# Attention in a two-layer backbone: a head's first scores ahead of the first projection group, and head norms in two buffers

## The chip, the cores and the metric

The kernel runs on one core of one Trainium2 chip, as one launch. The metric is device time in microseconds. One more execution was taken by the hardware profiler; its trace gives the start and end of each instruction on TensorE (PE for matmuls, PEld for weight loads), VectorE (DVE), ScalarE (ACT), GpSimd (POOL) and SyncE (SP, which issues all DMAs here).

## The reference

Two trunk layers, fp32, over 1024 latent and 256 context tokens of width 1024; layer 0 mixes tokens by differential attention, layer 1 by a state-space layer, and each is followed by an MLP. The change lies in layer 0's attention alone:

```python
q_l = apply_rope(heads_qk(q_l), cos, sin) * scale      # 8 heads, each with two 64-wide halves c
k_all = jnp.concatenate([k_c, k_l], axis=1)            # 1280 keys
s = jnp.einsum('bqhcd,bkhcd->bhcqk', q, k)
p = jax.nn.softmax(s, axis=-1)
w = p[:, :, 0] - lam * p[:, :, 1]                      # difference of two softmaxes
o = jnp.einsum('bhqk,bkhe->bqhe', w, v)
return rmsnorm(o, subln_g) * (1.0 - lambda_init)       # norm over each head's 128 outputs
```

Every product that needs fp32 accuracy is made of three reduced-precision ones (`mm3`, L132 to L134) of operands that `split` (L137 on ACT, L138 on POOL or DVE) cuts into a high and a low part.

## The kernel before

The attention phase (`phase_b`) runs over 72 units: 8 heads of 9 units. Unit 0 of a head holds the 256 context queries, which see 256 keys; units 1 to 8 hold 128 latent queries each, which see all 1280 keys. "(h, u)" below is unit u of head h. On PE, DVE, ACT and POOL the order is the order of the program text; on SP a scheduler sets it. Each engine executes in its own order, so an instruction that waits holds up all behind it on its engine.

The steps of one unit:

- `scores` (L517 in unit 0, L523 in the others) write products of queries Q and keys K to PSUM: banks 0 and 1 in unit 0, banks 0 to 4 otherwise.
- `maxima` on DVE (L532, L536) copy the scores to SBUF with their row maximum. `exps` on ACT (L543, L546) take exponentials and row sums, half c = 0 and then c = 1. `combine` on DVE (L554, L555, L557) forms the difference w.
- `w_part` on PE (L564, L569) transposes the w of the *previous* unit in three parts; part 0 goes to bank 5, part 2 to bank 7 where the unit has no projection group, else to bank 5. Part 0 is read by ACT L577 and DVE L578, the others by ACT L582 and, from a copy, POOL L583 and L584.
- `values` (L132 to L134 with 256 columns) multiplies a finished pair of units with V; `pair_out` (ACT L665, POOL L666) stores the result o to DRAM (`od`), `pair_sums` (PE L672, ACT L673) sums its squares.
- `proj_group` computes a sixth of the next head's Q or K: 24 products, a third of them at a time between the parts ("fills"). AHEAD says in which unit; unit 0 has two groups. The first, of context keys, is written out by ACT L464 and DVE L465 (`direct`). The others go through rotary steps: ACT L469, DVE L470, four row-moving DMAs (`FC<-FC`), POOL L475, DVE L478, and a split (ACT L137, DVE L138) whose DMAs store to DRAM (`Qd<-R`, `Kd<-R`). All groups use bank 7. Q and K are loaded back from DRAM (`R<-Qd`, `R<-Kd`); K's second half for the next head is asked for in unit 8, in a piece of 256 columns (128 KB) and one of 1024.

The head norm of a finished head h-1 runs during head h and head h+1. At the end of (h, 5) `norm_rows` transposes the inverse norms (PE L687), copies them (ACT L689) and writes them to DRAM (`rsd<-W`). For the five pairs of query blocks, in units 6, 7, 8, 0 and 1, `norm_load` asks at the start of the unit for the pair's o (`W<-od`) and for its norm rows spread over 128 partitions (`W<-rsd`). `norm_pair` at the *end* of the same unit multiplies them (DVE L697), splits the product (ACT L137, POOL L138, both `W<-W`) and stores it (`on<-W`). There is one set of buffers, in W.

Of the kernel before, what the change touches and what calls it, by code (L numbers as in the profile page):

```python
# [6 lines left out]
F32 = mybir.dt.float32  # L7
F32R = mybir.dt.float32r
# [5 lines left out]
KB = 256  # L14
# [56 lines left out]
class Prog:  # L71
# [369 lines left out]

        return split

    def proj_group(self, h, T, g, wt):

        nc = self.nc
        n, c0 = self.G_TOK[g], (256, 768, 0)[g]
        b = self.qb.next()[:, 0:n]
        scale = 1.0 if T else -0.125
        t = slice(c0 - 256, c0 + 256)  # L450
        hT = self.hT[g]
        q, sw, qc, s = self.rq, self.rs, self.rc, self.stg[:, :, 0:n]

        def product(k):
            return lambda: self.mm3(b, wt[k][0], wt[k][1], hT[0][:, k], hT[1][:, k], k == 0, k == 7)

        def out():
            dst = self.Kd if T else self.Qd
            for c in range(2):
                self.dma(dst[h % 2, c, :, c0 : c0 + n].rearrange("(l r) n -> r l n", l=2),  # L460
                         s[64 * c : 64 * c + 64].bitcast(F32))

        def direct():
            nc.scalar.activation(s[:, 0], b, AF.Copy, scale=scale)  # L464
            nc.vector.scalar_tensor_tensor(s[:, 1], b, scale, s[:, 0].bitcast(F32), ALU.mult, ALU.subtract)  # L465
            out()

        def evac():
            nc.scalar.activation(q, b, AF.Copy, scale=scale)  # L469
            nc.vector.scalar_tensor_tensor(qc, b, scale, self.cosT[:, t], ALU.mult, ALU.mult)  # L470
            for j in range(4):
                self.dma(sw[32 * j : 32 * j + 32], q[32 * (j ^ 1) : 32 * (j ^ 1) + 32])

        def sine():
            nc.gpsimd.tensor_tensor(sw, sw, self.sinT[:, t], ALU.mult)  # L475

        def add():
            nc.vector.tensor_tensor(qc, qc, sw, ALU.add)  # L478

        def store():  # L480
            self.split(s[:, 0], s[:, 1], qc)
            out()

        return [product(k) for k in range(8)], [direct] if g == 2 else [evac, None, sine, add, store]
# [135 lines left out]
    def phase_b(self):  # L620
# [59 lines left out]
            nc.vector.scalar_tensor_tensor(v, v, 1.0 / 128, tmp, ALU.mult, ALU.add)  # L680
            return lambda: self.rsqrt(rs, v)

        nob, nrb = self.wv(4, 256), self.wv(5, 256)
        nhi, nlo = self.wv(6, 256).bitcast(F32R), self.wv(7, 256).bitcast(F32R)

        def norm_rows(h):
            nc.tensor.transpose(pb[0:10, 384:512], hst[:, 2, h], self.ident)  # L687
            rT = nrb[0:10, 0:128]
            nc.scalar.activation(rT, pb[0:10, 384:512], AF.Copy)  # L689
            self.dma(self.rsd[h], rT)  # L690

        def norm_load(h, pair):
            self.dma(nob, self.od[h, :, 256 * pair : 256 * pair + 256])
            self.dma(nrb, self.rsd[h, 2 * pair : 2 * pair + 2].rearrange("a b -> (a b)").partition_broadcast(128))

        def norm_pair(h, pair):
            nc.vector.scalar_tensor_tensor(nob, nob, self.sg, nrb, ALU.mult, ALU.mult)  # L697
            self.split(nhi, nlo, nob, nc.gpsimd)
            for j, t in enumerate((nhi, nlo)):
                self.dma(self.on[h, j, :, 256 * pair : 256 * pair + 256], t.bitcast(F32))  # L700
# [94 lines left out]
        wts = {1: split(1)}  # L795
# [8 lines left out]
        def evac():  # L804
            while ready:
                self.w_evac(*ready.pop(0))

        with self.manual():
            for n in range(72 + 5):
                h, u = units[n] if n < 72 else (8, 9)  # L810
                front = n < 72
                groups = []
                pv = todo.pop(0)[1:] if todo and todo[0][0] == n else None
                late = pv and pv[1]
                parts = 3 if prev and prev[1] else 1 if prev else 0
                if front and n - 6 >= 9 and (n - 6) % 9 < 5 and (n - 6) // 9 < 7:
                    norm_load((n - 6) // 9 - 1, (n - 6) % 9)
                if h == 7 and u > 5:
                    load6(u)
                if front:  # L820
                    K = loaded[h, 'k', 0], loaded[h, 'k', 1]
                    pair = (u + 1) // 2
                    Q = loaded[h, pair]
                    s0 = hst[:, 0, h]
                    p, sn, sm = (p0.next(), p1), self.stat.next(), self.stat.next()
                    if u == 5 and h < 7:
                        load_v(h + 1)
                        load_k(h + 1, 0)
                    if u % 2 == 0 and u < 8 and (h, pair + 1) not in loaded:
                        load_q(h, pair + 1)  # L830
                    if h < 7:
                        groups = [self.proj_group(h + 1, *a, wts[a[0]]) for a in self.AHEAD.get(u, ())]
                    if len(groups) == 2:
                        for f in groups[0][0] + groups[0][1]:
                            f()
                    self.scores(u, Q, K)
                    if u == 8 and h < 7:
                        load_k(h + 1, 1)
                        load_q(h + 1, 0)
                        load_q(h + 1, 1)  # L840
                    self.maxima(u, p, sm)
                if front:
                    if h < 7:
                        if u == 0:
                            qsplit = self.proj_weights(h + 1, 0)
                        if u == 5 and h < 6:
                            ksplit = self.proj_weights(h + 2, 1)
                if 65 <= n < 75:
                    groups = [wo_group(wo_order[n - 65])]
# [7 lines left out]
                for part in range(3):  # L857
                    if part < parts:
                        tb = pb[:, 256:512] if part == 1 else self.bank(7 if part == 2 and not groups else 5)
                        t = self.w_part(prev[1], prev[2], part, tb)  # L860
                        ready.append((*t, part == 0))
                    if not late or part == 2:
                        evac()
                    if part == 1:
                        next_post()
                    if front and part < 2:
                        self.exps(u, part, p, sm, s0, sn)
                    if front and part == 1:
                        self.combine(u, p, s0, sn)
                    if late and part == 1:  # L870
                        evac()
                    if part == 0:
                        todo7, run7 = run7, []
                        for f in todo7:
                            f.pop(0)()
                            if f:
                                run7.append(f)
                    if part == (2 if n < 73 else 0):
                        while sums and sums[0][0] <= n:
                            sums.pop(0)[1]()  # L880
                    for f in fills[part]:
                        f()
# [19 lines left out]
                if 0 < h < 8:  # L902
# [3 lines left out]
                        newton()  # L906
                    elif u == 5:
                        norm_rows(h - 1)
                if h < 8 and n - 6 >= 9 and (n - 6) % 9 < 5 and (n - 6) // 9 < 7:
                    norm_pair((n - 6) // 9 - 1, (n - 6) % 9)  # L910
                if n == 72:
                    self.raw = Ring([self.wv(8, 1024), self.wv(12, 1024)])
                    self.wo_raws = [self.wo_load(3, 0), self.wo_load(0, 1)]
# [520 lines left out]
    def a_out(self, run, p, t):  # L1434
        self.dma(self.A0[run][p], t)
# [762 lines left out]
    def run(self):  # L2198
        tc = self.tc
        pool = lambda name, **kw: tc.tile_pool(name=name, bufs=1, **kw)  # L2200
        with pool("cst") as self.cst, pool("psp", space=bass.MemoryType.PSUM) as psp, \
# [22 lines left out]
            with pool("r0") as rp, pool("fc") as cp:  # L2224
                self.R, self.F = rp.tile([128, 59 * KB], F32R, name="R0"), cp.tile([128, 8 * KB], F32, name="FC")
                with pool("f0") as fp, pool("sp") as sp:
                    self.F0, self.SP = fp.tile([128, 41 * KB], F32, name="F0"), sp.tile([128, 12 * KB], F32, name="SP")
                    self.f0 = lambda off, *dims: self.view(self.F0, off, dims)
                    self.setup()
                    self.lam_setup()  # L2230
                    more = [self.view(self.SP, 4 * i, (1024,)) for i in range(3)]
                    self.raw = Ring([self.wv(4 * i, 1024) for i in range(4)] + [self.f0(24.5 + 4 * i, 1024) for i in range(4)] + more)
                    self.phase_v()
                with pool("r1") as rp, pool("f1") as fp:
                    self.R1, self.F1 = rp.tile([128, 20 * KB], F32R, name="R1"), fp.tile([128, 21 * KB], F32, name="F1")
                    self.phase_b()
                for g in range(3):
                    for j in range(2):
                        self.dbg(f"oT{g}{j}", self.oT[g][j].bitcast(F32))
                if self.stop == "B":  # L2240
                    return
# [69 lines left out]
```

## Time and profile before

| | |
|---|---|
| median of 3 runs | 2927.47 us (2924.79 to 2931.78) |
| profiled execution | 2919.65 us, of it 2917.8 us span |
| mean granted TensorE clock | 0.983 |
| attention phase in the span | from 221.28 us (first L517) to about 877 us |
| PE, DVE, ACT, POOL busy | 94%, 69%, 47%, 36% of the span |

In the rows of the profile, `L132 PE MATMUL PS<-H,R` is line, engine, operation, and what is written from what. `[2.56 <-ACT F L582]` is idle time of that engine before the instruction and what ended it. A row of waits reads: who waited, for whom, total us, times, longest. A row of stretches reads: from:to, us, then busy time of PE, PEld, DVE, ACT and POOL with their instruction counts (or of one engine alone), granted TensorE clock, DMA share, GB/s.

### The profile page before, as it was taken

Reading aid. Unit: us, or ns where it says so; the run is one execution under the profiler, and the core shown is the slowest. Engines: PE = TensorE matmul, PEld = TensorE weight load, DVE = VectorE, ACT = ScalarE, POOL = GpSimd, SP = SyncE. Lnnn points to the kernel's source line nnn. Section 1 sums busy time; section 2 is a strip of 40 time slices with the busy share of each in tenths; the row PEclk is TensorE's granted clock in tenths of the full one; section 3 lists DMA queues with packets and bytes.
Section 4 is the critical chain, followed back from the end, with each engine's and each line's share of the span. In section 5 each row is a group of like instructions: output and inputs, shape, how many; then the busy total and the mean of one; then the engine's idle time right before and its main releaser. Section 6 shows DMA issues by size and latency. Waiting matters only on the chain.

```text
span 2917.8 us, 43645 instructions
## 1 busy us (share of the span) xinstructions
PE 2739.2 (94%) x15201; PEld 2287.3 (78%) x15201; DVE 2021.4 (69%) x2957; ACT 1369.8 (47%) x2556; POOL 1063.4 (36%) x923
## 2 busy tenths in 40 slices
PE   6999999999899999999999999688899899999999
PEld 4787888878777887878877778588788688878887
DVE  5457777777764576767697868699743787758566
ACT  3425655555553753333443435377543643345443
POOL 3314666666653600000020004499310443326324
PEclk9999999999999999999999999899999999999999
DMA  9955555555735448886799988468834254467544
GB/s 299 307 171 159 151 174 166 170 157 152 236 117 166 132 164 314 295 301 221 244 293 278 276 247 253 148 202 276 270 130 131 72 183 157 148 212 254 165 134 141
DMA packets 452010, 588.43 MB, mean 202 GB/s; under 512 B 60622, under 2 KB 297420, under 8 KB 448588
## 3 DMA queue, kind: packets, MB, share of 16 engines
q1 hardware_dynamic: 451788, 585.63, 63.6%
q8 instruction: 120, 1.97, 0.3%
q14 instruction: 102, 0.84, 0.1%
HBM read 398.47 MB, written 182.82 MB: 199 GB/s over the span
## 4 chain that ended last, share of the span: by engine, by line
PE 62%; DMA 12%; DVE 12%; issue 6%; ACT 3%; POOL 3%; SPq 2%; DVEq 0%; POOLq 0%; ACTq 0%
PE PS L132 18%; PE PS L134 17%; PE PS L133 17%; SPq L80 2%; DMA FU<-in_mlp_w 2%; PE PS L523 2%; PE PS L1802 2%; ACT F L546 1%; DMA Ta<-FU 1%; PE PS L1837 1%; DVE H L138 1%; PE PS L569 1%; DVE F L536 1%; DVE R L138 1%; DMA U<-in_mlp_w 1%
## 5 line engine op out<-in xcount | busy, mean ns | idle before, releaser
L132 PE MATMUL PS<-H 128*128 128x512 f32 x1048 | 411.9, 394 | 7.3 <-DVE FD L1609 5.0
L134 PE MATMUL PS<-H 128*128 128x512 f32 x1048 | 409.8, 392 | 1.1 <-DVE H L138 1.1
L133 PE MATMUL PS<-H 128*128 128x512 f32 x1048 | 410.7, 392 | 0.0
L132 PE MATMUL PS<-H,R 128*128 128x512 f32 (+1 forms) x836 | 310.9, 377 | 18.6 <-ACT F L582 13.7
L133 PE MATMUL PS<-H,R 128*128 128x512 f32 (+1 forms) x836 | 303.9, 364 | 1.1 <-POOL H L138 1.1
L134 PE MATMUL PS<-H,R 128*128 128x512 f32 (+1 forms) x836 | 303.3, 363 | 0.0
L132 PEld LDWEIGHTS PS<-H 128*128 128x128 f32 x1048 | 197.7, 189 | 51.8 <-DVE FD L1609 5.3
L134 PEld LDWEIGHTS PS<-H 128*128 128x128 f32 x1048 | 197.7, 189 | 43.9 <-DVE H L138 1.5
L133 PEld LDWEIGHTS PS<-H 128*128 128x128 f32 x1048 | 197.8, 189 | 41.5 <-issue 1.3
L137 ACT ACTIVATE R<-W 128x512 fp32r<-128x512 f32 (+1 forms) x199 | 138.7, 704 | 185.4 <-PE PS L133 112.9
L546 ACT ACTIVATE F<-F,stat 128x1280 f32<-128x1280 f32 x128 | 174.4, 1362 | 84.3 <-DVE F L536 84.1
L132 PE MATMUL PS<-R,H 128*128 128x512 f32 x532 | 212.3, 401 | 1.4 <-ACT R L137 1.4
L133 PE MATMUL PS<-R,H 128*128 128x512 f32 x532 | 209.7, 394 | 0.0
L134 PE MATMUL PS<-R,H 128*128 128x512 f32 x532 | 207.6, 394 | 0.2 <-POOL H L138 0.2
L137 ACT ACTIVATE H<-U 128x640 fp32r<-128x640 f32 x216 | 132.8, 677 | 152.1 <-PE PS L133 114.6
L132 PEld LDWEIGHTS PS<-H,R 128*128 128x128 f32 x836 | 160.5, 193 | 47.8 <-ACT F L582 15.1
L138 DVE TENSOR_TENSOR H<-W,H 128x512 fp32r<-128x512 f32 (+1 forms) x137 | 128.9, 952 | 96.7 <-ACT H L137 95.7
L138 DVE TENSOR_TENSOR H<-U,H 128x640 fp32r<-128x640 f32 x216 | 163.1, 791 | 42.0 <-ACT H L137 42.0
L536 DVE TENSOR_SCALAR_CACHE_REDUCE F<-PS 128x1280 f32<-128x1280 f32 x128 | 185.1, 1483 | 8.6 <-PE PS L523 8.3
L138 DVE TENSOR_TENSOR R<-W,R 128x512 fp32r<-128x512 f32 (+1 forms) x164 | 149.1, 916 | 57.3 <-ACT R L137 49.5
L583 POOL TENSOR_SCALAR R<-F 128x256 fp32r<-128x256 f32 (+1 forms) x128 | 123.8, 967 | 169.9 <-ACT F L582 148.7
L134 PEld LDWEIGHTS PS<-H,R 128*128 128x128 f32 x836 | 160.6, 192 | 26.2 <-POOL R L138 1.0
(488 smaller groups left out, 6830.6 us busy)
## 6 DMA issues: line engine op xcount, KB each, us to landing
W<-in_mlp_w SPq DMA_DIRECT2D x184, 256.0 KB, 3.1
U<-Aa SPq DMA_DIRECT2D x108, 320.0 KB, 4.8
Aa<-FU SPq DMA_DIRECT2D x91, 320.0 KB, 4.6
Ad<-F SPq DMA_DIRECT2D x112, 256.0 KB, 2.6
W<-Ad SPq DMA_DIRECT2D x112, 256.0 KB, 2.7
FU<-in_mlp_w SPq DMA_DIRECT2D x32, 512.0 KB, 6.1
Ta<-FU SPq DMA_DIRECT2D x16, 1024.0 KB, 4.8
recd<-U SPq DMA_DIRECT2D x64, 256.0 KB, 4.5
```

The costliest lines, as they stand in the source:

```text
L80: return self.nc.sync.dma_start(out=out, in_=in_)
L132: mm(out, ah, bh, start=first, stop=False, **kw)
L133: mm(out, ah, bl, start=False, stop=False, **kw)
L134: mm(out, al, bh, start=False, stop=last, **kw)
L137: self.nc.scalar.activation(hi, src, AF.Copy)
L138: (lo_eng or self.nc.vector).tensor_tensor(lo, src, hi.bitcast(F32), ALU.subtract)
L523: mm(self.PS[:, 1280 * c + k0 : 1280 * c + k1], Q[:, c, r, qs], K[c][:, k0:k1], start=r == 0, stop=r == 1)
L536: ts(p[c], self.PS[:, 1280 * c : 1280 * c + 1280], 1.0, None, ALU.mult, ALU.min, accum_out=sm[:, c : c + 1])
L546: nc.scalar.activation(p[c], p[c], AF.Exp, bias=sm[:, c : c + 1], scale=-1.0, accum_out=sn[:, 0:1] if c else s0[:, u + 1 : u + 2])
L569: self.nc.tensor.transpose(tb[:, 128 * (kt - k0) : 128 * (kt - k0) + 128], w[:, 128 * kt : 128 * kt + 128], self.ident)
L583: nc.gpsimd.tensor_scalar(hi, t, 1.0, 0.0, ALU.mult, ALU.add)
L1802: mm(b[:, o : o + 160], X[:, d, i, 64 * j : 64 * j + 128], U[:, 4 * n + i, cols], start=True, stop=True)
```

## The change

1. In unit 0 the head's scores stand first on PE, and the products of the first group follow; that group is written to bank 4 instead of bank 7. Its `direct` step follows `maxima`.
2. The norm's loaded buffers and its split buffers exist twice, the second set in F1 (4.5 KB more per partition). The inverse norms are copied to a place of their own there.
3. The loads of pairs 1 to 4 are asked for one unit earlier, at the start of the unit ahead of that of their `norm_pair`; the load of pair 0 stands at the end of (h, 5), behind `norm_rows`.
4. `norm_pair` moves from the end of its unit to the middle, behind `exps` of c = 1 and ahead of `combine`.

```diff
-    def proj_group(self, h, T, g, wt):
+    def proj_group(self, h, T, g, wt, bank=None):
...
-        b = self.qb.next()[:, 0:n]
+        b = (self.qb.next() if bank is None else bank)[:, 0:n]
...
-        nob, nrb = self.wv(4, 256), self.wv(5, 256)
-        nhi, nlo = self.wv(6, 256).bitcast(F32R), self.wv(7, 256).bitcast(F32R)
+        nbufs = [(self.wv(4, 256), self.wv(5, 256))] + [(self.view(self.F1, 21 + 2 * i, (256,)), self.view(self.F1, 22 + 2 * i, (256,)))
+                                                        for i in range(1)]
+        nsplit = [(self.wv(6, 256).bitcast(F32R), self.wv(7, 256).bitcast(F32R))] + \
+                 [tuple(self.view(self.F1, 23 + i, (256,)).bitcast(F32R) for i in range(2))]
+        (nob, nrb), nbuf = nbufs[0], Ring(range(2))
+        nloaded = []
...
         def norm_load(h, pair):
-            self.dma(nob, self.od[h, :, 256 * pair : 256 * pair + 256])
...
+            i = nbuf.next()
+            nloaded.append(i)
+            self.dma(nbufs[i][0], self.od[h, :, 256 * pair : 256 * pair + 256])
...
         def norm_pair(h, pair):
+            i = nloaded.pop(0)
+            (nob, nrb), (nhi, nlo) = nbufs[i], nsplit[i]
...
-                if front and n - 6 >= 9 and (n - 6) % 9 < 5 and (n - 6) // 9 < 7:
-                    norm_load((n - 6) // 9 - 1, (n - 6) % 9)
+                if front and n - 6 >= 9 and (n - 6) % 9 < 4 and (n - 6) // 9 < 7:
+                    norm_load((n - 6) // 9 - 1, (n - 6) % 9 + 1)
...
-                        groups = [self.proj_group(h + 1, *a, wts[a[0]]) for a in self.AHEAD.get(u, ())]
+                        groups = [self.proj_group(h + 1, *a, wts[a[0]], self.bank(4) if a == (1, 2) else None)
+                                  for a in self.AHEAD.get(u, ())]
+                    self.scores(u, Q, K)
                     if len(groups) == 2:
-                        for f in groups[0][0] + groups[0][1]:
+                        for f in groups[0][0]:
                             f()
-                    self.scores(u, Q, K)
...
                     self.maxima(u, p, sm)
+                    if len(groups) == 2:
+                        groups[0][1][0]()
...
                     if front and part == 1:
+                        if n - 6 >= 9 and (n - 6) % 9 < 5 and (n - 6) // 9 < 7:
+                            norm_pair((n - 6) // 9 - 1, (n - 6) % 9)
                         self.combine(u, p, s0, sn)
...
                     elif u == 5:
                         norm_rows(h - 1)
-                if h < 8 and n - 6 >= 9 and (n - 6) % 9 < 5 and (n - 6) // 9 < 7:
-                    norm_pair((n - 6) // 9 - 1, (n - 6) % 9)
+                        if h < 7:
+                            norm_load(h - 1, 0)
```

More of the change, by code (lines that the diff above doesn't have):

```diff
@@ L681, in norm_calc @@
             return lambda: self.rsqrt(rs, v)
-        nob, nrb = self.wv(4, 256), self.wv(5, 256)
-        nhi, nlo = self.wv(6, 256).bitcast(F32R), self.wv(7, 256).bitcast(F32R)
+        nbufs = [(self.wv(4, 256), self.wv(5, 256))] + [(self.view(self.F1, 21 + 2 * i, (256,)), self.view(self.F1, 22 + 2 * i, (256,)))
[4 more added lines that the diff above has]
+        nloaded = []
         def norm_rows(h):
             nc.tensor.transpose(pb[0:10, 384:512], hst[:, 2, h], self.ident)
-            rT = nrb[0:10, 0:128]
+            rT = self.view(self.F1, 25, (128,))[0:10]
             nc.scalar.activation(rT, pb[0:10, 384:512], AF.Copy)
@@ L692, in norm_load @@
         def norm_load(h, pair):
-            self.dma(nob, self.od[h, :, 256 * pair : 256 * pair + 256])
-            self.dma(nrb, self.rsd[h, 2 * pair : 2 * pair + 2].rearrange("a b -> (a b)").partition_broadcast(128))
+            i = nbuf.next()
+            nloaded.append(i)
+            self.dma(nbufs[i][0], self.od[h, :, 256 * pair : 256 * pair + 256])
+            self.dma(nbufs[i][1], self.rsd[h, 2 * pair : 2 * pair + 2].rearrange("a b -> (a b)").partition_broadcast(128))
         def norm_pair(h, pair):
+            i = nloaded.pop(0)
+            (nob, nrb), (nhi, nlo) = nbufs[i], nsplit[i]
             nc.vector.scalar_tensor_tensor(nob, nob, self.sg, nrb, ALU.mult, ALU.mult)
@@ L2234, in run @@
                 with pool("r1") as rp, pool("f1") as fp:
-                    self.R1, self.F1 = rp.tile([128, 20 * KB], F32R, name="R1"), fp.tile([128, 21 * KB], F32, name="F1")
+                    self.R1, self.F1 = rp.tile([128, 20 * KB], F32R, name="R1"), fp.tile([128, int(25.5 * KB)], F32, name="F1")
                     self.phase_b()
```

## The prediction

> **What bounds the kernel now.** I read the page first, then who waited for whom inside the attention phase, then one head in order of time, engine by engine.
>
> ```profile
> span 2917.8 us, 43645 instructions
> PE 2739.2 (94%) x15201; PEld 2287.3 (78%) x15201; DVE 2021.4 (69%) x2957; ACT 1369.8 (47%) x2556; POOL 1063.4 (36%) x923
> ...
> PE PS L569 <- DVE R L578: 20.2, 15, 2.7
> PE PS L132 <- ACT F L582: 13.7, 6, 2.6
> ...
> DVE W L697 <- DMA W<-rsd: 30.3, 14, 4.4
> ```
>
> PE is the bound, and what can be won is its idle time. In the attention phase it waits 13.7 us for L582: that is the first group, six times, because the previous unit's part 2 still occupies bank 7. The waits for L578 come from DVE, which itself stood 30.3 us before L697 for the norm rows. Both are what the change aims at. The ceiling is thus a few tens of us of 2919.65.
>
> The stretches from (h, 6) to (h+1, 3), for h = 1 to 5 and, last, (6, 6) to (7, 3), hold nearly all of it; the first time in each row is its length:
>
> ```profile
> 348.49:405.69 57.20, 51.88 (x329) 45.70 (x327) 43.78 (x70) 32.47 (x67) 34.75 (x35) 1.00 0.59 173
> 430.84:487.61 56.77, 53.14 (x328) 47.15 (x327) 42.28 (x70) 32.57 (x67) 34.99 (x35) 0.97 0.59 174
> 512.77:570.75 57.98, 53.34 (x329) 47.16 (x328) 43.37 (x70) 32.10 (x67) 34.74 (x35) 0.97 0.57 170
> 595.95:654.00 58.05, 53.16 (x328) 47.13 (x327) 43.45 (x70) 32.58 (x67) 34.79 (x35) 0.97 0.62 171
> 679.19:736.83 57.64, 52.06 (x329) 45.70 (x328) 42.91 (x70) 32.45 (x67) 34.75 (x35) 1.00 0.60 172
> 762.01:824.99 62.98, 47.67 (x275) 41.96 (x274) 43.02 (x68) 32.08 (x64) 35.48 (x34) 0.86 0.79 249
> ```
>
> The first five average 57.5 us. I follow head 1; its PE, in order of time:
>
> ```profile
> 355.51 2.56 PE L523 MATMUL PS<-R,R 128*128 128x512 f32 x12
> 357.91 0.60 PE L569 MATMUL PS<-ident,F 128*128 128x128 f32 x4
> 374.69 0.39 PE L132 MATMUL PS<-H,R 128*128 128x256 f32 x1 [2.56 <-ACT F L582]
> 377.67 1.12 PE L517 MATMUL PS<-R,R 128*128 128x256 f32 x8
> 380.05 0.50 PE L132 MATMUL PS<-H,R 128*128 128x512 f32 x1 [0.83 <-DVE R L465]
> 386.82 2.47 PE L523 MATMUL PS<-R,R 128*128 128x512 f32 x12
> 397.27 0.39 PE L133 MATMUL PS<-R 128*128 128x256 f32 x1 [1.50 <-DVE R L578]
> ```
>
> Unit 7 begins at 355.51, the next head's scores at 377.67, its unit 1 at 386.82. Three waits stand there: 2.56 for bank 7, 0.83 for L465 (the same bank, second group), 1.50 in unit 2.
>
> **The change, part by part.**
>
> *The order in unit 0.* The group loses its wait for bank 7: bank 4 is free once `maxima` of unit 8 are done, ahead of PE's arrival. Gone are 2.56 and 0.83. PE does the same 32 matmuls in the other order, so nothing is added there. What is late next is what the scores need.
>
> *Pair 0 of the norm, the step I weigh most.* Its rows are written at the end of unit 5 and read back in unit 6. The built program has L697 of pair 0 behind the two L536 of unit 6 and ahead of L554. In the kernel before, it came after L578:
>
> ```profile
> 351.59 1.49 DVE L536 TENSOR_SCALAR_CACHE_REDUCE F<-PS 128x1280 f32<-128x1280 f32 x1
> 354.61 0.16 DVE L554 RECIPROCAL stat<-stat 128x1 f32<-128x1 f32 x1 [1.52 <-ACT F L546]
> 356.53 0.69 DVE L578 TENSOR_TENSOR R<-PS,R 128x512 fp32r<-128x512 f32 x1
> 357.24 0.75 DVE L697 SCALAR_TENSOR_TENSOR W<-W,lamc 128x256 f32<-128x256 f32 x1
> 365.71 1.23 DVE L138 TENSOR_TENSOR R<-FC,R 128x512 fp32r<-128x512 f32 x1
> ...
> 604.86 0.58 DVE L697 SCALAR_TENSOR_TENSOR W<-W,lamc 128x256 f32<-128x256 f32 x1 [0.19 <-DMA W<-rsd]
> ...
> 353.61 0.54 SPq L80 DMA_DIRECT2D W<-rsd  x1
> ...
> W<-rsd SPq DMA_DIRECT2D x35, 128.0 KB, 4.0
> ```
>
> The rows' read is issued at 353.61 and, at a median of 4.0 us to landing, is there at about 357.2 to 357.6; head 4's L697, at the same place, still waited 0.19. Nothing in the change brings this read forward: it stands behind the same row-moving DMAs and the same write. So DVE, done with L536 at 353.1, now stands until 357.2, and `combine` of unit 6, queued behind, goes with it. From 357.2: L697 about 0.5, then the 2.6 us that L554 to the end of L578 took (354.61 to 357.22): 360.3. PE's first transposes of unit 7 (357.91) need that w and bank 5, which L578 frees: a new wait of 2.4 us. ACT is held too: the norm's copy stands ahead of L577 and of the L582 behind it, and POOL's L583 follows those.
>
> *What that delays, and the keys.* On POOL and DVE:
>
> ```profile
> 356.10 0.79 POOL L583 TENSOR_SCALAR R<-F 128x256 fp32r<-128x256 f32 x1 [4.99 <-ACT F L582]
> 360.38 1.30 POOL L475 TENSOR_TENSOR FC<-FC,W 128x512 f32<-128x512 f32 x1
> 361.71 1.77 DVE L478 TENSOR_TENSOR FC<-FC 128x512 f32<-128x512 f32 x1 [0.30 <-POOL FC L475]
> ...
> 289.93 1.27 SPq L80 DMA_DIRECT2D Qd<-R  x2
> 291.30 2.74 SPq L80 DMA_DIRECT2D FC<-FC  x4
> 294.14 1.02 SPq L80 DMA_DIRECT2D R<-Kd  x2
> ...
> R<-Kd SPq DMA_DIRECT2D x14, 128.0 KB, 2.3
> ```
>
> L554 moves from 354.61 to about 357.6, hence L577, L582, L583 and L475 by the same 3.0, L478 with them; L697 of pair 1, now ahead of `combine` of unit 7, adds its 0.75: the store split L138 ends at 370.6 instead of 366.9. In the changed program's SP order the 256 key columns that `scores` of unit 0 read stand behind that store and the four FC moves, as they did at head 0 already; at heads 1 to 5 they stood ahead. From store to issue is 4.2 us (289.93 to 294.14), landing 2.3 more: 377.1. PE, 2.4 late, is ready at 372.1 + 2.4 = 374.5. New wait: 2.6 us, in place of the 2.56. Before, the group's products covered that load; now they stand behind the scores.
>
> So scores start at 377.1. Until unit 1 PE has what took 12.1 us (374.69 to 386.82) less the 0.83: 11.3; another head took slightly less, I take 11.1. Unit 1 begins at 388.2, 1.4 late. In unit 2 the 1.50 goes: L578 there is not later, because the L697 that stood ahead of `maxima` is gone, and PE arrives late itself. With DVE's wait for pair 4's rows gone too (the loads are a unit ahead now), unit 3 begins 0.7 earlier than before, averaged over the heads. Five heads: -3.5 us.
>
> *The clock.* A wait also costs afterwards. Consecutive stretches, PE busy first, granted clock second:
>
> ```profile
> 369.70:373.11 3.41, 2.42 (x22) 1.00 0.68 219
> 455.03:458.45 3.42, 1.42 (x12) 1.00 0.72 137
> 458.45:461.86 3.41, 3.41 (x19) 0.50 0.93 279
> ```
>
> PE idle 2.0 of 3.41 us was followed by 3.41 us at half clock; idle 1.0 was not. A wait of 2.5 us, wherever it begins, puts 2.0 into one such stretch about half the time ((3.41 + 2.5 - 4.0) / 3.41 = 0.56). Half clock costs 1.7 us of PE work. In unit 7 the wait for keys hides it; behind that wait nothing does. Half of five: +4.3; the three 0.97 stretches above, hardly longer than the other two, already hold 0.5. Net +3.8. (The Trainium skill, "TensorE: Matmul & The Clock Gate", section "HAM oscillation", warns of idle gaps beyond about 3.4 us alone; by it these waits cost nothing afterwards, and the sum would be 3.8 lower. The trace has half clock after PE waits of 2.5 us, so I charge it.)
>
> *Head 0's start.* There the group ran while Q was loading:
>
> ```profile
> 222.76 1.68 PE L517 MATMUL PS<-R,R 128*128 128x256 f32 x7 [1.13 <-DMA R<-Qd]
> ```
>
> Now it follows: its 2.98 us (374.69 to 377.67 at full clock) come onto PE's path, less about 0.7 of waits of its own that it had there: +2.3. I take that near the 0.83 of its wait for L465 in head 1. Bounds: 0 if the waits of units 1 and 2 absorb it, 4 at half clock.
>
> *Head 0 to 1.* No norm runs there; the group's wait for bank 7 gives way to one for the keys, 294.14 + 2.3 = 296.4, about when bank 7 came free: 0.
>
> *Head 6 to 7.*
>
> ```profile
> 775.13 0.49 DVE L697 SCALAR_TENSOR_TENSOR W<-W,lamc 128x256 f32<-128x256 f32 x1 [4.40 <-DMA W<-rsd]
> 779.10 0.96 PE L569 MATMUL PS<-ident,F 128*128 128x128 f32 x4 [2.72 <-DVE R L578]
> 801.51 0.98 PE L672 MATMUL PS<-lamc,adat 128*128 128x1 f32 x4 [6.44 <-ACT F L582]
> ```
>
> The rows land at 775, so unit 7's wait grows by about 4; in return the 6.44 in head 7's unit 0 shrinks, as its L697 finds its rows. I take 0, within 3 either way: no row shows POOL, busy there, without its waits.
>
> *Sum:* 2.3 - 3.5 + 3.8 = +2.6 us on the profiled execution: 2919.65 + 2.6 = 2922.3. The runs' median, 2927.47, is 7.8 above that execution; I add the same 2.6: **2930 us**.
>
> **The rivals.**
>
> *A: the keys come in time.* DVE's pairs of waits shrink (L697 took 0.49 to 0.75, L478 could run in 0.7 instead of 1.77), or the short key load lands before PE is ready. Then a head saves the 2.6, unit 1 starts early and unit 2's waits vanish entirely: 3.7 a head, 18.5 in all, less 2.3: 2911. For it: the key load has only 2.6 us to make up. Against: it hangs behind a store on DVE that the norm moves back.
>
> *B: the rows also come in time,* so that pair 0 costs nothing: 28 us won, 2899. Against it speaks the 0.19 wait at 604.86; only an earlier read could do it, and the change has none.
>
> *C: slower, by the queue behind the store and the half clock after it.* Each us by which L138 or the FC moves are later holds the keys and all of unit 0 by as much. At one more us per head and half clock behind every wait for keys: 5 + 8.5 - 0.5 - 3.5 + 2.3 = +12: 2939. It decides from the point where keys land later than about 378 in head 1's time. For it: three of six such waits before already led to half clock, and other loads crowd SP there. Against: unit 2's waits still give some back.
>
> **How the numbers follow.** 0.2% is about what a measurement of this kernel can tell from no change: 5.9 us, so 2921.6 to 2933.3 counts as the same. Forecast 0.40, A 0.21, B 0.06, C 0.33. Faster is A and B, 0.27; same 0.40; slower 0.33. The forecast's own range is 2922 to 2934. For eight in ten I leave out B and the far end of C: low, A gives 2911; high, C with head 6 at +3 and 1 for rounding gives 2943.
>
> **What would show it.** Right: L697 of pair 0 idle about 4 us for its rows ahead of L554; PE waiting 2 to 3 us at unit 7's first L569 and again at L517 for `R<-Kd`; no wait of the first group for L582; none of L697 in unit 2. Wrong: PE passing from unit 8 into L517 without a wait (A), or unit 7's transposes on time (B); stretches of head 1 to 5 above 59 us with clock 0.95 or less (C).

## The result, and the profile after

| | before | changed |
|---|---|---|
| median of 20 runs each | 2927.31 us | 2938.30 us |
| ratio to before, 95% interval | | 1.0035 (1.0024 to 1.0047) |
| span of the profiled execution | 2917.8 us | 2931.8 us |
| attention phase, first L517 to the scores of (7, 8) | 653.9 us | 662.3 us |

The changed kernel is slower by 0.35%, about 10 us. The two profiled executions differ by 14.0 us, of which 8.4 lie in the attention phase. What lies outside that phase is the same program, and its part of the span ranges from 2257 to 2277 us over the thirteen kernels profiled here, in no order that follows an edit; so from here on each kernel's profile is read by the length of its attention phase, and its time by the ratio of its runs. Each phase length is that of one execution; how much it varies between executions of one kernel, no run here shows.

The first lines of the changed kernel's page. PE is busy 2.2 us more than before, DVE 6.8 us less: 11.8 of the extra 14.0 us of span are idle time of PE.

```profile
span 2931.8 us, 43649 instructions
...
PE 2741.4 (94%) x15201; PEld 2288.7 (78%) x15201; DVE 2014.6 (69%) x2957; ACT 1367.6 (47%) x2556; POOL 1071.3 (37%) x923
```

Who waited for whom in the attention phase (total us, times, longest; here and below from 221 to 877 us of the trace). L705 is the norm's product, L697 before.

```profile
PE PS L569 <- DVE R L578: 29.7, 14, 7.7
...
DVE F L705 <- DMA F<-rsd: 19.8, 3, 9.6
...
DVE W L705 <- DMA W<-rsd: 12.6, 3, 4.3
...
PE PS L133 <- DVE R L578: 11.5, 6, 3.7
PE PS L517 <- DMA R<-Kd: 11.1, 6, 2.6
...
ACT R L137 <- DMA Kd<-R: 8.9, 5, 2.2
```

The row of the first group's wait for L582 (13.7 us before) is gone. In its place stand 11.1 us for the key load, and L569's wait has grown from 18.6 to 29.7 (the 20.2 of the prediction is for a longer window, 217 to 900). DVE still waits 32.4 us for norm rows (before: 30.3): the second set of buffers has not shortened that, it has left fewer and longer waits (6 for 14), and they stand where `combine` stands behind them.

The stretches from (h, 6) to (h+1, 3), as before: five of them now average 59.4 us (57.5 before), and the last takes 65.43.

```profile
347.33:407.72 60.39, 53.78 (x329) 47.03 (x327) 43.20 (x71) 32.03 (x67) 35.43 (x35) 0.97 0.56 164
432.29:491.32 59.03, 52.03 (x328) 45.76 (x327) 43.18 (x71) 32.04 (x67) 35.44 (x35) 1.00 0.56 168
515.92:575.38 59.46, 53.25 (x328) 46.79 (x327) 43.08 (x71) 32.16 (x67) 35.36 (x35) 0.97 0.58 167
600.01:659.46 59.45, 53.19 (x328) 46.78 (x327) 43.63 (x71) 32.15 (x67) 35.35 (x35) 0.97 0.56 167
684.10:742.88 58.78, 53.24 (x329) 46.96 (x328) 43.17 (x71) 32.02 (x67) 35.40 (x35) 0.97 0.57 168
767.45:832.88 65.43, 49.06 (x275) 42.43 (x274) 45.19 (x68) 31.78 (x64) 37.05 (x34) 0.84 0.78 243
```

Head 1 in the changed kernel, engine by engine (start, duration, what it is, idle time before it and what ended it):

```profile
355.93 0.48 DVE L705 SCALAR_TENSOR_TENSOR W<-W,lamc 128x256 f32<-128x256 f32 x1 [4.00 <-DMA W<-rsd]
356.33 0.16 DVE L554 RECIPROCAL stat<-stat 128x1 f32<-128x1 f32 x1
...
358.99 0.66 PE L569 MATMUL PS<-ident,F 128*128 128x128 f32 x4 [2.08 <-DVE R L578]
...
369.91 1.28 SPq L80 DMA_DIRECT2D Qd<-R  x2
371.29 2.74 SPq L80 DMA_DIRECT2D FC<-FC  x4
374.13 1.26 SPq L80 DMA_DIRECT2D R<-Kd  x2
...
376.56 0.98 PE L517 MATMUL PS<-R,R 128*128 128x256 f32 x6 [2.57 <-DMA R<-Kd]
...
398.32 0.39 PE L133 MATMUL PS<-R 128*128 128x256 f32 x1 [1.63 <-DVE R L578]
```

Read down: DVE stands 4.00 us for pair 0's rows, and L554 of `combine` follows it; PE waits 2.08 for the L578 at the end of that chain; the store `Qd<-R` and the four row moves go out ahead of `R<-Kd`; PE waits 2.57 for those keys; and in unit 2, where the prediction saw no wait, PE still waits 1.63. That last wait has its own chain, on ACT and DVE in unit 1:

```profile
388.66 0.63 ACT L137 ACTIVATE R<-FC 128x512 fp32r<-128x512 f32 x1 [2.21 <-DMA Kd<-R]
...
389.33 0.69 DVE L138 TENSOR_TENSOR R<-FC,R 128x512 fp32r<-128x512 f32 x1 [2.47 <-ACT R L137]
...
390.74 1.48 DVE L536 TENSOR_SCALAR_CACHE_REDUCE F<-PS 128x1280 f32<-128x1280 f32 x1
```

ACT's split L137 of the next store writes the staging buffer `stg`, and there the first group's context keys still lie until their store `Kd<-R` has read them. DVE's half of the split waits for ACT, and unit 1's `maxima` (L536) stand behind it in DVE's order.

### The profile page after: what moved, and what is told of

Read it like the earlier page. It is cut to its first block, busy times and chain, and to the rows that moved or that the text cites. A ratio compares the mean times of both kernels' runs of the same rounds, so it can differ in the third digit from the quotient of the medians.

```text
span 2931.8 us, 43649 instructions
## 1 busy us (share of the span) xinstructions
PE 2741.4 (94%) x15201; PEld 2288.7 (78%) x15201; DVE 2014.6 (69%) x2957; ACT 1367.6 (47%) x2556; POOL 1071.3 (37%) x923
## 4 chain that ended last, share of the span: by engine, by line
PE 63%; DMA 13%; DVE 9%; POOL 5%; issue 4%; ACT 3%; SPq 2%; ACTq 0%; DVEq 0%; POOLq 0%
PE PS L132 18%; PE PS L134 18%; PE PS L133 18%; SPq L80 2%; PE PS L523 2%; PE PS L1815 2%; PE PS L569 1%; PE PS L1850 1%; DMA FU<-in_mlp_w 1%; DMA Ta<-FU 1%; DVE H L138 1%; DMA Kd<-R 1%; ACT F L546 1%; POOL R L583 1%; DVE F L557 1%
## 5 line engine op out<-in xcount | busy, mean ns | idle before, releaser
L137 ACT ACTIVATE R<-W 128x512 fp32r<-128x512 f32 (+1 forms) x199 | 138.8, 705 | 183.3 <-PE PS L133 116.9
L137 ACT ACTIVATE H<-U 128x640 fp32r<-128x640 f32 x216 | 132.7, 677 | 150.8 <-PE PS L133 114.2
L536 DVE TENSOR_SCALAR_CACHE_REDUCE F<-PS 128x1280 f32<-128x1280 f32 x128 | 185.2, 1483 | 8.9 <-PE PS L523 8.3
L133 PEld LDWEIGHTS PS<-H,R 128*128 128x128 f32 x836 | 160.7, 192 | 27.8 <-POOL H L138 6.8
L132 PEld LDWEIGHTS PS<-H,R 128*128 128x128 f32 x836 | 160.4, 192 | 27.1 <-issue 4.1
L134 PEld LDWEIGHTS PS<-H,R 128*128 128x128 f32 x836 | 160.3, 192 | 25.6 <-issue 0.8
```

Of the source, the lines that this page charges most:

```text
L132: mm(out, ah, bh, start=first, stop=False, **kw)
L133: mm(out, ah, bl, start=False, stop=False, **kw)
L134: mm(out, al, bh, start=False, stop=last, **kw)
L137: self.nc.scalar.activation(hi, src, AF.Copy)
L536: ts(p[c], self.PS[:, 1280 * c : 1280 * c + 1280], 1.0, None, ALU.mult, ALU.min, accum_out=sm[:, c : c + 1])
```

## The experiments

The theory held after the comparison, **N**, has two parts: pair 0's product stands ahead of `combine` without its rows, and the 256 key columns come too late for the scores. A third, **G**, was added after the first four kernels below: the group's later place makes its staging buffer come free late. The main rival to N was **S**: putting the scores first exposes the key load whatever the norm does. Phase lengths are from the first L517 to the scores of (7, 8); it is 653.9 in the kernel before. Each kernel's ratio is to runs of the kernel before made beside its own.

| kernel | ratio to before (95%) | phase, us |
|---|---|---|
| changed | 1.0035 (1.0024 to 1.0047) | 662.3 |
| order and bank alone | 1.0004 (0.9987 to 1.0021) | 656.7 |
| norm half alone | 1.0008 (0.9992 to 1.0025) | 659.6 |
| changed, keys early | 1.0050 (1.0033 to 1.0066) | 665.1 |
| changed, rows written a unit earlier | 0.9969 (0.9953 to 0.9985) | 649.1 |
| before, bank 4 alone | 0.9964 (0.9952 to 0.9976) | 644.5 |
| changed, norm a unit later | 0.9919 (0.9907 to 0.9931) | 629.6 |
| changed, own staging | 1.0012 (1.0003 to 1.0020) | 654.9 |
| changed, keys early and own staging | 0.9994 (0.9982 to 1.0005) | 648.2 |
| all three: norm later, keys early, own staging | 0.9905 (0.9882 to 0.9928) | 621.8 |
| the same, inverse norms in one unit | 0.9892 (0.9871 to 0.9912) | 622.0 |
| old order, bank 4, norm later | 0.9921 (0.9896 to 0.9946) | 629.6 |

**The two halves.** First the order and the bank alone, on the kernel before:

```diff
-                        groups = [self.proj_group(h + 1, *a, wts[a[0]]) for a in self.AHEAD.get(u, ())]
+                        groups = [self.proj_group(h + 1, *a, wts[a[0]], self.bank(4) if a == (1, 2) else None)
+                                  for a in self.AHEAD.get(u, ())]
+                    self.scores(u, Q, K)
                     if len(groups) == 2:
-                        for f in groups[0][0] + groups[0][1]:
+                        for f in groups[0][0]:
                             f()
-                    self.scores(u, Q, K)
...
                     self.maxima(u, p, sm)
+                    if len(groups) == 2:
+                        groups[0][1][0]()
```

> The order of unit 0 and bank 4 alone; the norm as in the kernel before. Theory N (the loss comes from the norm half: pair 0's product ahead of combine without its rows, and the later place of the key load on SP that goes with it): the first group's waits in unit 8 (13.7 us in all) and the two of 0.83 go, the 256 key columns stay ahead of the store on SP and land about 368 in head 1's time, so the scores of unit 0 wait for nothing; head 0's start adds 1.9. About 10 to 14 us faster than before, 2913 to 2917. Rival S (scores ahead of the group expose the key load whatever the norm does): a wait of 1.5 to 2.5 us at L517 in each of six heads takes the place of the one removed; 2926 to 2930.

Measured: no difference from before, so both were wrong in part. The time is the one S gave, but its cause is not there: the scores of heads 2 to 6 pass without a wait for keys, because their load stands ahead of the store on SP in this kernel. Theory N fails on the gain. The waits of this kernel, and SP and PE at head 1's end:

```profile
ACT R L137 <- DMA Kd<-R: 20.8, 5, 4.7
...
PE PS L569 <- DVE R L578: 18.0, 13, 2.5
...
PE PS L133 <- DVE R L578: 10.6, 6, 3.3
...
PE PS L523 <- DVE F L536: 8.7, 12, 2.3
...
PE PS L517 <- DMA R<-Kd: 0.9, 1, 0.9
```

```profile
365.78 0.32 SPq L80 DMA_DIRECT2D R<-Kd  x1
367.13 1.27 SPq L80 DMA_DIRECT2D Qd<-R  x2
...
383.59 1.07 PE L523 MATMUL PS<-R,R 128*128 128x512 f32 x4
...
392.36 1.19 PE L523 MATMUL PS<-R,R 128*128 128x512 f32 x4 [2.27 <-DVE F L536]
```

PE reaches unit 1 at 383.59 instead of 386.82, 3.2 us early, and loses it there: unit 2's scores wait 2.27 for unit 1's `maxima`, which follow the split that waits for `Kd<-R`. ACT waits 20.8 us in all for that store, against 8.9 in the changed kernel. G came from these rows and those of the early keys, below.

The norm half alone (the changed kernel with unit 0 as before, and bank 7):

```diff
-                        groups = [self.proj_group(h + 1, *a, wts[a[0]], self.bank(4) if a == (1, 2) else None)
-                                  for a in self.AHEAD.get(u, ())]
+                        groups = [self.proj_group(h + 1, *a, wts[a[0]]) for a in self.AHEAD.get(u, ())]
+                    if len(groups) == 2:
+                        for f in groups[0][0] + groups[0][1]:
+                            f()
                     self.scores(u, Q, K)
-                    if len(groups) == 2:
-                        for f in groups[0][0]:
-                            f()
...
                     self.maxima(u, p, sm)
-                    if len(groups) == 2:
-                        groups[0][1][0]()
```

> The norm half alone (two buffers, loads a unit ahead, the product in the middle of the unit); unit 0 as in the kernel before, the first group on bank 7 and ahead of the scores. Theory N: PE waits 2.1 to 3.6 us at unit 7's first transposes in heads 1 to 5 and 7 to 8 in head 6, the first group's waits of about 2.5 stay, units 3 and 5 give back 0.6 a head and head 7's unit 0 about 5: 5 to 12 us slower than before, 2932 to 2939. Rival S: the norm half costs nothing or gains, 2920 to 2928.

```profile
PE PS L569 <- DVE R L578: 28.3, 14, 8.1
...
PE PS L132 <- ACT F L582: 11.9, 6, 2.8
```

Measured 1.0008, which can't be told from no change: it is the time that S gave, and its interval reaches into N's 5 to 12 us, so the time doesn't decide. N's waits are there, and in the phase they cost 5.7 us. At unit 7 PE waits 19.4 us in six heads (20.8 in the changed kernel), and the first group's wait stays (11.9, before 13.7). No wait for keys appears, since the group's products cover their load. The halves cost 2.8 and 5.7 us of phase, about the change's 8.4 together, but not out of the same waits: the wait for keys (11.1 us) exists only with both, because the order takes away its cover and the norm half its place on SP.

**The keys, taken away.** The 256 columns get a buffer of their own, and their load is asked for in unit 7 instead of unit 8:

```diff
+        kx = self.view(self.R1, 20, (256,))
+
+        def load_kx(h):
+            self.dma(kx.bitcast(F32), self.Kd[h % 2, 1, :, 0:256])
...
+                    if u == 7 and h < 7:
+                        load_kx(h + 1)
...
-                    self.scores(u, Q, K)
+                    self.scores(u, Q, (K[0], kx) if u == 0 and h else K)
```

> The changed kernel with one more buffer of 1 KB per partition: the 256 key columns of the second half that unit 0 reads are loaded into it by a DMA of their own, units earlier; the rest as it is. Theory N with its second part right: the waits at L517 (11.1 us in six heads) go, those at unit 7 stay: 8 to 12 us less than the changed kernel, about 2927 to 2930, level with the kernel before. Rival S: the whole loss goes and more, 2915 to 2925. If the wait only moves to unit 1 or 2: no change from 2938.

```profile
PE PS L569 <- DVE R L578: 29.6, 18, 6.9
...
ACT R L137 <- DMA Kd<-R: 18.0, 5, 4.1
...
PE PS L132 <- ACT FC L670: 5.6, 6, 0.9
...
PE PS L523 <- DVE F L536: 4.4, 10, 1.0
```

The row for L517 is gone, and the time isn't less: the third case named, the wait moves. Unit 0 starts early, ACT waits for the staging 18.0 us instead of 8.9, and in unit 2 PE waits 5.6 us for L670 and 4.4 for `maxima` (0.9 and 0.7 in the changed kernel). A wait of 11.1 us on the engine that bounds was worth nothing by itself. (The Trainium skill, "Perfetto Trace Analysis", section "Optimization Strategy", advises to find the gaps on the bound engine and make what blocks them start sooner. Here that removed the gap and left the time, as the next dependency was due just behind.)

**The rows, in time.** The inverse norms are finished and written one unit earlier:

```diff
                     if u == 3:
-                        newton = norm_calc(h - 1)
+                        norm_calc(h - 1)()
                     elif u == 4:
-                        newton()
-                    elif u == 5:
                         norm_rows(h - 1)
-                        if h < 7:
-                            norm_load(h - 1, 0)
+                    elif u == 5 and h < 7:
+                        norm_load(h - 1, 0)
```

> The changed kernel with the inverse norms finished and written out one unit earlier (end of unit 4 instead of 5), so that pair 0's rows can land before unit 6; pair 0's load stays at the end of unit 5. Theory N: DVE's idle time before pair 0's product goes, with it PE's waits at unit 7 (2.1 to 3.6 us in five heads, 7.7 in head 6, of which 2.7 were there before); the waits at L517 stay near 2: 14 to 19 us less than the changed kernel, 2919 to 2924. Rival S: unit 7 on time but the time lost again at L517, under 5 us less, 2933 to 2938.

```profile
PE PS L691 <- ACT FC L665: 14.9, 6, 2.5
...
PE PS L517 <- DMA R<-Kd: 12.8, 6, 2.7
...
PE PS L569 <- DVE R L578: 2.4, 2, 1.9
```

N confirmed, and a new bill: L569 waits 2.4 us in all instead of 29.7, and DVE waits for no rows. But the transposes of `norm_rows` (L691), now in a unit that also writes out a pair, wait 2.5 us each, 14.9 in all, and the waits for keys are now followed by half clock in all of heads 2 to 6. With that the phase is 649.1, 13 less than changed; in runs it is 0.9969 against 1.0035, about 19.

The other way to the same end is to need the rows later: all five products one unit later.

```diff
-                        if n - 6 >= 9 and (n - 6) % 9 < 5 and (n - 6) // 9 < 7:
-                            norm_pair((n - 6) // 9 - 1, (n - 6) % 9)
+                        if n - 7 >= 9 and (n - 7) % 9 < 5 and (n - 7) // 9 < 7:
+                            norm_pair((n - 7) // 9 - 1, (n - 7) % 9)
```

(and the loads of pairs 1 to 4 likewise)

> The changed kernel with all five products of the norm, and the loads of pairs 1 to 4, one unit later (pair 0's product in unit 7); pair 0's load stays at the end of unit 5. Theory N: the rows have landed, PE's waits at unit 7 (2.1 to 3.6 us, 7.7 in head 6) go; the waits at L517 stay: 14 to 19 us less than the changed kernel, 2919 to 2924, as with the rows written earlier. Rival: pair 0 in unit 7 holds VectorE ahead of the store split, keys come later still, under 8 us less, above 2930.

```profile
PE PS L569 <- DVE R L578: 11.4, 9, 2.1
...
PE PS L517 <- DMA R<-Kd: 10.0, 6, 2.3
```

0.9919, well beyond both expectations: faster than before by 0.8%. The phase is 32.7 us shorter than the changed kernel's, of which the waits at unit 7 are only 20.8 (13.1 in heads 1 to 5, 7.7 in head 6). The expectation left out the clock: PE is at half clock for 22.4 us of the phase here and for 37.5 in the changed kernel. The 17.1 us that began in unit 7 there are all gone, with 2.0 more elsewhere: 15.1 less, an estimated half of that in time, 7.5. Another 3.3 are waits in head 7's unit 2 (1.57 instead of 4.84), 1.1 fewer for keys.

**The bank without the order.** The kernel before, with its first group on bank 4 and still ahead of the scores:

```diff
-                        groups = [self.proj_group(h + 1, *a, wts[a[0]]) for a in self.AHEAD.get(u, ())]
+                        groups = [self.proj_group(h + 1, *a, wts[a[0]], self.bank(4) if a == (1, 2) else None)
+                                  for a in self.AHEAD.get(u, ())]
```

> The kernel before with one edit: the first group of unit 0 goes to bank 4; its products stay ahead of the scores. Theory G (what the order half loses, it loses because the group comes later: the context keys are staged and stored 3 to 4 us later from the one staging buffer, the split of the next store waits for that DMA, VectorE waits for the split and takes unit 1's maxima late): without the new order the staging is earlier, not later, so the waits for bank 7 (15.4 us) go and little comes in their place: 8 to 14 us faster than before, 2911 to 2917. Rival: units 1 and 2 are bound by VectorE in any case, the 2.5 us come back there, under 4 us gained, 2921 to 2925.

0.9964, in G's range. One of the change's two parts in unit 0 is a gain of 0.36%, and the other spends it: the order costs 12 us of phase (656.7 beside 644.5). The wait on the staging agrees with G, at a third of the 20.8 us with the order:

```profile
ACT R L137 <- DMA Kd<-R: 7.1, 3, 2.5
```

**The staging.** The changed kernel with a buffer of its own for the first group's result:

```diff
         q, sw, qc, s = self.rq, self.rs, self.rc, self.stg[:, :, 0:n]
+        if bank is not None:
+            s = self.view(self.R1, 20, (2, 256))
```

> The changed kernel with one more buffer of 2 KB per partition: the first group's result is staged there, so the split of the next store does not wait until it has been written out. Theory G: ScalarE's wait for the key store (2.2 us in head 1), VectorE's 2.5 behind it and PE's 1.6 in unit 2 go: 5 to 9 us less than the changed kernel, 2929 to 2933. Rival: the 1.6 in unit 2 is the chain of maxima, exponentials and combine, timed from unit 1's own scores; it stays, 2936 to 2940.

```profile
PE PS L571 <- DVE R L580: 27.1, 14, 5.9
...
PE PS L519 <- DMA R<-Kd: 14.1, 6, 3.0
...
PE PS L133 <- DVE R L580: 6.0, 6, 3.7
```

Head 3's unit 1 and its first `maxima`:

```profile
471.13 2.49 PE L525 MATMUL PS<-R,R 128*128 128x512 f32 x12
...
472.73 1.49 DVE L538 TENSOR_SCALAR_CACHE_REDUCE F<-PS 128x1280 f32<-128x1280 f32 x1
```

(Lines are two higher here: L571 is L569, L519 is L517, L525 is L523, L538 is L536.) The row of ACT's wait for `Kd<-R` is gone, and unit 2's wait, 1.26 to 1.63 in the changed kernel, falls to 0.23 or 0.24 in heads 2, 3, 5 and 6; in head 4 it is 1.40. `maxima` begin 1.60 us after unit 1's scores in those four heads (472.73 less 471.13), in the changed kernel 2.63 to 3.40. 1.0012 against 1.0035: G holds, the rival doesn't. With the early keys as well:

> The changed kernel with both buffers, the 256 key columns loaded early and the first group's own staging. The early keys alone gave nothing (2939). Theory G: they gave nothing because the staging was next in line; with both the waits at L517 and those of 3.6 us in units 1 and 2 go together: 15 to 20 us less than with the keys alone, 2919 to 2925. Rival: something else in units 1 and 2 binds, no more than 5 us less, 2934 or above.

```profile
PE PS L571 <- DVE R L580: 30.2, 16, 5.5
...
PE PS L133 <- DVE R L580: 7.7, 6, 1.6
```

0.9994 against 1.0050 with the keys alone, 16 us: the keys are worth something once the staging isn't next in line. In part the rival holds too: with the scores this early, 1.6 us in unit 2 come back in four of five heads. ACT no longer waits for the staging there; in head 2 DVE is at work without a gap on unit 0's `combine` and the split until `maxima` begin, 3.2 us after unit 1's scores (391.03 less 387.81), so DVE's own work is now next in line.

**All three, and a version that beats both kernels.**

> The changed kernel with the norm one unit later and both buffers (keys early, own staging). If the three causes add up, the waits at unit 7, at L517 and most of those in unit 2 are gone: against the norm one unit later alone, whose waits at L517 are 1.7 us and in unit 2 1.4 us a head, 6 to 12 us less, 0.988 to 0.990 of the kernel before. Rival (PE is now held in units 1 and 2 by the chain of maxima, exponentials and combine whatever comes first): no more than 3 us less, 0.991.

```profile
PE PS L571 <- DVE R L580: 10.8, 9, 1.7
...
PE PS L133 <- DVE R L580: 9.3, 6, 1.6
```

0.9905 of before lies between the expectation and its rival and can't be told from the 0.9919 of the later norm alone; the phase, 7.8 us shorter, speaks for the expectation. The waits at unit 7 and for keys are gone, those in unit 2 are not: PE still waits 1.6 there in each of heads 2 to 6, and 1.2 in unit 5. For the latter, both steps of the inverse norms were put at the end of unit 3, as in the kernel with early rows, where unit 5 had no wait:

> The same, with both steps of the inverse norms (sum and reciprocal root) at the end of unit 3 instead of units 3 and 4. PE's wait of 1.2 us in unit 5 (before: 1.5), which comes from VectorE's steps at the end of unit 4, goes in six heads: 5 to 7 us less than the kernel without this edit. Rival: it moves to unit 4, no change.

The phase is the same (622.0 and 621.8), and unit 5 waits 1.21 as before: the expectation was wrong. In the kernel with early rows, where that wait was missing, unit 4 was 2.9 us longer (9.9 for 7.0), which is a likely reason that no run here tests. The ratio, 0.9892, can't be told from 0.9905. Last, the old order in unit 0 with the later norm and no buffer for keys or staging:

> No new buffer for keys or staging, the old order in unit 0: group to bank 4 and ahead of the scores; norm one unit later, both steps of the inverse norms at the end of unit 3. With the old order the key load lies behind the group's products and the staging is early, so nothing need be bought for them: the gain of the bank alone (9 us) and that of the later norm (14 to 19 us against the changed kernel, of which 4 to 5 against the kernel before) and 6 for unit 5 add up: 0.990 to 0.994 of the kernel before. If it is below that, the old order is the better one.

0.9921, in the range, but not by its sum: the 6 us for unit 5 had just failed, and the staging was not free either, since ACT waits 14.7 us for `Kd<-R` here. The phase is that of the new order with the later norm (629.6 both). With the norm later and without the two extra buffers, the order of unit 0 thus shows no difference; with them the new order is 7.8 us of phase ahead.

## Why the prediction was right or wrong

The time lies within the range given, and slower by more than 0.2% had 0.33; but the likeliest case said no change, 2930, and the time is 8 us above it and outside that case's own 2922 to 2934. C's number was 2939. Its mechanism did not decide, so that agreement is luck: C asked for keys after 378 in head 1's time, and PE went on with them before 377. C's sign came true by half: four of the five stretches are above 59 us, but none has a clock of 0.95 or less.

*Pair 0 ahead of `combine`: right.* L705 idle 4.00 ahead of L554, PE's wait at unit 7 2.08, 2.71, 2.37, 3.59 and 2.37 in heads 1 to 5, mean 2.6 for a forecast of 2.4. The kernels with the rows earlier or the product later showed that the rows are its cause. The Trainium skill, "TensorE: Matmul & The Clock Gate", section "Architectural detail: the array is 16× 32×32, not 1× 128×128", calls ACT and DVE strict first-in-first-out; these rows agree: L554 stands behind the waiting L705, and counted from the start of its unit it runs at 9.0 us (356.33 less 347.33), in the kernel before at 6.1 (354.61 less 348.49).

*The keys behind store and row moves: right as a wait, wrong as a price.* 2.57, 2.43, 2.21, 1.41 and 1.54, mean 2.0 for 2.6. Unit 1 began 2.1 us late against its head's unit 6, not 1.4, partly because the 0.83 of L465 that I deducted had been there in two of the five heads alone. But the keys alone, taken away, gave nothing.

*Unit 2: the step that failed.* "In unit 2 the 1.50 goes: L578 there is not later" was to make unit 3 begin 0.7 earlier; without the later term for the clock, that is 2.1 won between units 1 and 3. Measured, unit 3 begins 1.9 later, so 0.2 was won: 1.9 short in each head, 9 us in five (the clock's part is in both measured figures). L578 was later. The first row is of the kernel before, the second of the changed one:

```profile
396.53 0.69 DVE L578 TENSOR_TENSOR R<-PS,R 128x512 fp32r<-128x512 f32 x1
...
397.59 0.68 DVE L578 TENSOR_TENSOR R<-PS,R 128x512 fp32r<-128x512 f32 x1
```

I followed the group on PE, but not what its result does next, its `direct` step, its store and the one staging buffer behind it. The own-staging kernel shows that: unit 1 begins as late there as in the changed kernel (40.8 us after its head's unit 6, beside 40.7), but 1.8 us are then won up to unit 3, near the 2.1 forecast. A smaller error adds to it: the norm's product left the place ahead of `maxima`, but it now stands between `maxima` and L578, and from the one to the other DVE takes 6.85 us instead of 6.40 in every head.

*The clock: +3.8 forecast, about +1.7 found.* In heads 1 to 5 there are four half-clock stretches where there were three. The working held: three of five waits at unit 7 were followed by one (the fourth followed a wait in unit 2), and the wait for keys then took up part of it (1.41 to 2.21 in those heads, 2.43 and 2.57 in the others). None followed a wait for keys, where I had charged half of five, so the term came out smaller by where the stretches fell. In the kernel with early rows one followed the wait for keys in all five of heads 2 to 6, with own staging in one. Head 3's at unit 7 of the changed kernel, in consecutive stretches:

```profile
521.89:525.30 3.41, 3.41 (x24) 1.00 0.55 157
525.30:528.71 3.41, 1.04 (x7) 1.00 0.35 91
528.71:532.13 3.42, 3.42 (x11) 0.50 0.35 111
```

PE is idle for 2.37 of 3.41 us, and 3.42 us at half clock follow. The Trainium skill, "TensorE: Matmul & The Clock Gate", section "HAM oscillation", warns of idle gaps beyond about 3.4 us; the trace again differs, as this gap is 2.37 us long, and the measurement decides.

*Small terms.* Head 0 to unit 1 of head 1: forecast +2.3, measured -1.1, of which 0.5 is the phase's earlier start. Unit 0 is 1.9 longer, but head 0's unit 2 gave back more than that: its wait is 1.40 instead of 2.47, and the half-clock stretch of 3.41 us that stood there, worth an estimated 1.7, is gone. So it came out below the lower bound of 0. Units 3 to 5 of heads 2 to 6 gave 0.6 each that I had not counted. Head 6 to 7: +2.5, inside the 3 either way.

## What to carry to other kernels

When work is moved behind other work, follow its result to the buffers it holds: a single staging buffer whose store ends later can hold up an engine that has nothing to do with the move. Data loaded from DRAM and consumed in the middle of an in-order queue must be there with room to spare, or be consumed a stage later: here that one unit was worth 1.2% of the whole kernel. And a wait on the bound engine is worth its length only if nothing else is due behind it: test it together with the next one in line before giving it up or paying for it.

## What was not expected of the hardware

That waits cost again by the clock was in the prediction; its size across a phase was not: the later norm saved 20.8 us of PE waits at unit 7, and with them went 17.1 us at half clock, by estimate another 8.5 us. What sets such a stretch off shows more sharply over all thirteen traces than in the prediction's two examples. The granted clock steps on a grid of 3.41 us, and in the attention phases from head 0's unit 1 on, each of the 73 full-clock stretches of that grid in which PE was idle for more than 1.8 us was followed by half clock. None with less than 1.6 was, and between the two it went either way, 6 times of 22.
